# Windowed attention and retention: products of two heads of 64 issued in turn

## The chip, the cores and the metric
The kernel runs on one core of one Trainium2 chip. TensorE (PE in the profile; its loads of stationary operands are PEld) multiplies, VectorE (DVE) and ScalarE (ACT) do the elementwise work, GpSimd (POOL) some more of it, and SyncE (SP) issues the DMAs. Each engine works through its own instructions in the order in which they stand in the program. The metric is the device time of one execution, in microseconds (us).

## The reference
Two layers of a transformer block over 512 latent tokens and 256 context tokens, width 1024. A layer is a gated feed-forward, a mixer of four groups of four heads of 64 features, and a second feed-forward. The change touches two of the four groups. Group A is attention of 128 queries over the 256 context keys and a window of latent key blocks, and the context's own queries over the context keys; group C is retention in both directions:

```python
# group A, per block of 128 queries: keys of the context and of the blocks n-1, n, n+1
s = q @ k.T / 8 ; p = softmax([s, sink]) ; o = p @ v
# group C, per chunk of 128 tokens, forwards and (flipped) backwards
att = einsum('bnihd,bnjhd->bnhij', qc, kc) * d_intra[None, None]
o_intra = einsum('bnhij,bnjhe->bnihe', att, vc)
u = einsum('bnjhd,hj,bnjhe->nbhde', kc, k_w, vc)      # state after each chunk: decay * s + u
o_cross = einsum('bnihd,hi,nbhde->bnihe', qc, q_w, s_prev)
return (o_intra + o_cross), s_final
```

The last layer needs no outputs of the context stream, so it has 4 blocks of queries where the first layer has 6.

## The kernel before
The streams stay on chip by feature, so a tile of 128 partitions holds two heads of 64 features, one in partitions 0 to 63 and one in 64 to 127. Large products (feed-forwards `ul` and `y`, the mixer's projections `pj`) run as three float32r passes; the products of the heads run in float32, and the trace shows each of these as two matmul instructions.

A mixer (`mixer`) first runs retention for two pairs of heads (`group_c`, j = 0 and 1), then projects groups A and B (`proj_ab`), then runs the windowed attention of group A (`attend`), beside which nine more projections are issued, and then the recurrence of group D with group B's attention (`attend2`) in it. The order on each engine is made when the program is built: a scheduler walks the instructions by priority, which is the order of the code unless `tc.high_priority(offset=...)` shifts it, and puts projections (`pj`) between the small products where these have to wait. PSUM banks are handed out by tag (`psum`), within a tag in the order of the code: `ptr` and `ms` have one bank each in this part, `pj` three, `po` one, and `pS` holds one tile of two banks (`S`, or `ro` in retention).

In `attend` the loop is over t (two tiles of queries), blocks n, and the two heads hf of the tile. For one head: scores `S` (L1017 through the helper `mm`), maximum on DVE (L1032), exponential on ACT (L1036), scaling on DVE (L1040), transposes into `ptr` (L1047), their copy into `PT` by ACT (L1048), and then the products with the values, L1050: 4 or 5 for a latent block (the one or two neighbours, the block itself and two context blocks), 2 for a context block. They write the head's 64 partitions of the bank `w` (`po` in the rows), so each uses 64 of the array's 128 columns.

In `group_c` the loop at the end is over blocks b and the two heads e. For one head: the scores `ra` in the bank `ptr` (L1213, 64 features in, 128 columns out), their product with the decay mask `at` on DVE for both directions (L1215), and for each direction the product with the values (L1219, 128 rows in, 64 columns out) and the product of the state `St` with the weighted queries `qw` (L1221, 64 rows in, 64 columns out), both into the head's partitions of `ro`. The states come from sums `su` (L1194) in the bank `ms`, one after the other, which stand in the code ahead of this loop. The recurrence's part already has products of two heads in turn: L1117 and L1123 (`po` and `z` under L1069 in the rows) in `attend_pair`, with the same use of `high_priority`, and L595, where the two directions read partitions 0 to 63 and 64 to 127 and write two banks (tag `gr`).

Of the kernel before, what the change touches and what calls it, by code (L numbers as in the profile page):

```python
"""Two layers of a hybrid flow-matching backbone, on one core.

The streams stay on chip by feature, x[feature, token], latent tokens before context tokens. Large products
run as three float32r passes over operands split exactly into two parts of 12 bits; the others in float32.
"""
# [11 lines left out]
F32 = mybir.dt.float32  # L17
# [24 lines left out]
# how far the background work's priority lies behind that of the work around it  # L42
# [21 lines left out]
def more_constants():  # L64
# [3 lines left out]
    # rotary: partner of each feature and the sign it enters with  # L68
# [14 lines left out]
    # retention  # L83
# [18 lines left out]
    # window masks: keys of the block before, of the block after  # L102
# [11 lines left out]
class Whole:  # L114
# [20 lines left out]
    def columns(self, rows, name):  # L135
        """Rows of 128 values in DRAM, as columns on chip."""
# [44 lines left out]
    def mod_direct(self, l, b, bufs):  # L181
        """Four columns of the modulation of both streams, as rows in four groups side by side."""
# [18 lines left out]
    def mod_block(self, l, b):  # L201
        """The same, summed over rows on the vector engine."""
# [15 lines left out]
    def mod_sum(self):  # L218
        """The sum over partitions of the block before."""
# [21 lines left out]
    def scales(self, l, n, v):  # L241
        """Per feature: the norm's gain with the modulation's scale."""
        nc = self.nc
        g = self.const.tile([128, KT], F32, name=f"gs{l}{n}{v}")
        o = (3 * n + 1) * KT
        nc.vector.scalar_tensor_tensor(out=g, in0=self.mod[l][v][:, o:o + KT], scalar=1.0,
                                       in1=self.ng[:, (3 * l + n) * KT:(3 * l + n + 1) * KT], op0=ALU.add, op1=ALU.mult)
        return g
# [12 lines left out]
    def rsqrt(self, x, n, eps, op=ALU.add, scale=None):  # L261
        """(x op eps) ** -0.5 of n columns: a first guess from the bits, three steps of Newton's."""
# [16 lines left out]
    def rstd(self, segs=SEGS):  # L279
        """The rows' factors, by token."""  # L280
# [11 lines left out]
    def spread(self, pt, cols):  # L292
        """Rows of 128 tokens from columns, on all partitions or one for each 64."""
# [3 lines left out]
    def spread_rows(self, r, segs):  # L297
        """Rows over all partitions, in two banks."""
# [6 lines left out]
    def raw_open(self, l, n, shifts=True):  # L305
        """Products with modulate(rms_norm(x)) from products with x by gain: the rows' factors and the shifts enter after them.
        The shifts are two more columns, between the streams."""
# [12 lines left out]
    def raw_tile(self, k):  # L320
        """One finished tile of x by gain, in two parts of 12 bits."""
# [7 lines left out]
    def raw_rows(self, pool):  # L329
        """The rows' factors of both streams on all partitions."""  # L330
# [4 lines left out]
    def ready(self, l, n):  # L335
        """What to do with each finished tile of x before norm n of layer l."""
# [7 lines left out]
    def norm_mod(self, l, n, segs=SEGS):  # L344
        """h = modulate(rms_norm(x)), in two parts of 12 bits."""
# [15 lines left out]
    def mm3(self, outs, wh, wl, xh, xl, segs, first, last):  # L361
        """outs[i] += w.T x over segs, from parts; the low parts' product is below float32."""
# [8 lines left out]
    def split(self, raw, shape, tag, pool=None, bufs=None):  # L371
        """The two parts of a tile."""
# [8 lines left out]
    def ffn(self, l, i, segs, chunks, background, last_cb):  # L381
# [4 lines left out]
        for ci, cn in enumerate(chunks):  # L386
            gs = []
            wo = self.raw.tile([128, cn, D], F32, name="wo", tag="wo", bufs=1)
            for j in range(cn):
# [8 lines left out]
                # the first products do not wait for the shifts  # L398
# [51 lines left out]
    def gates(self, l, n, segs, half):  # L450
        """The gate columns; made once the modulation is there."""
# [8 lines left out]
    def rw_cols(self, l):  # L460
# [34 lines left out]
        # 1 - mu; 1 - k_a / 2; 2 ln_b  # L495
# [13 lines left out]
    def scan_ap(p, d, o, n, shift):  # L509
        """Tokens o to o + n, context first, in the order of direction d, or the tokens before them."""  # L510
# [33 lines left out]
    def rw_low(self, pw, pa):  # L544
        """tanh of the decays' and the inputs of the rates' low-rank part, in the order of each direction."""
# [9 lines left out]
    def rw_lengths(self, p):  # L555
        """One over the lengths of the removal keys, as columns of [block, direction, head]."""
# [18 lines left out]
    def rw_decay(self, u, p):  # L575
        """Decays, rates and removal keys of 128 tokens of each direction, for both pairs of heads."""
# [33 lines left out]
        # half the removal key of length one  # L610
# [8 lines left out]
    def rw_ops(self, u, st, p, has_r):  # L619
        """Operands of the chunks, and the products of their rows, head by head."""  # L620
# [46 lines left out]
    def rw_late(self, u, st, bon, has_r):  # L667
        """What the steps need besides the products: keys and values by token; and the bonus, in the order of the tokens."""
# [32 lines left out]
    def block(d, u):  # L701
        """The block of tokens, context first, that direction d reaches at step u."""
        return u if d == 0 else (1 - u if u < 2 else 7 - u)

    def rw_inverse(self, ops):
        """(1 - A)^-1 of every chunk, transposed, in the place of A: blocks of 16 by substitution, then twice the block beside."""
# [63 lines left out]
    def rw_step(self, ops, c, S, Y, has_r, first):  # L770
        """One chunk of both directions: its outputs, and the states after it."""
# [46 lines left out]
    def rw_norm(self, Y):  # L818
        """The head norm of each token's outputs, without its gain."""
# [10 lines left out]
    def rw_out(self, Y, u, bon):  # L830
        """Adds the normed outputs, by feature, in the order of the tokens."""
# [12 lines left out]
    def rw_scan(self, p, bon, ctx_out, first):  # L844
        """The recurrence, 128 tokens at a time; the next operands are made while a chain runs. `first` goes in after the first decays."""
# [39 lines left out]
    def psum_open(self, ctx, **tags):  # L885
        """Banks by use: within a tag they are handed out in the order of the program."""
# [3 lines left out]
    def h_open(self, n=T + 2):  # L890
        """The operands of a phase's products, by feature, in two parts: they outlive the phase that makes them."""
# [14 lines left out]
    def first_mods(self):  # L906
        """The first norm's gains, then its shifts, through buffers that are still free."""
# [16 lines left out]
    def proj(self, l, cols, both, evac):  # L924
        """128 columns of the projection (as (first, count) runs) of the latent tokens or of both streams."""
# [576 lines left out]
```

## Time and profile before
| what | value |
|---|---|
| timed runs | 3579.98 us median of 3 (3574.42 to 3582.41) |
| profiled execution | span 3572.8 us from its first to its last instruction |
| busy: PE, PEld, DVE, ACT, POOL | 3416.8 (96%), 2759.6 (77%), 2003.8 (56%), 1145.2 (32%), 168.4 (5%) us |
| chain that ended last | PE 84%, DVE 9%, ACT 3% of the span |
| mean granted TensorE clock | 0.983 |

The page gives the profiled execution's own time as its span; the timed runs also hold what lies around the span, and their fastest is 1.6 us above it, their median 7.2 us. A matmul's duration in the trace reaches from its start to its last result, and the next one starts earlier than that; so what a matmul costs TensorE is read from the distance between two starts, not from the duration.

### The profile page before, as it was taken

How to read it: one execution, taken by the hardware profiler on the slowest of the kernel's cores; microseconds unless marked ns; L12 is line 12 of the kernel's file. 1: busy time of each engine (PE TensorE's matmuls, PEld its weight loads, DVE VectorE, ACT ScalarE, POOL GpSimd, SP SyncE). 2: the span in 40 equal slices, each digit the busy share in tenths (PEclk: the TensorE clock that was granted, in tenths of full speed). 3: DMA queues.
4: the chain of work that ended last, by engine and by line, in shares of the span. 5: the costliest groups of instructions: out<-in, count | busy, mean ns of one | idle time of the engine just before them, and what ended most of it. 6: DMA issues, size and time to landing. Idle time of an engine off the chain costs nothing.

```text
span 3572.8 us, 54928 instructions
## 1 busy us (share of the span) xinstructions
PE 3416.8 (96%) x22756; PEld 2759.6 (77%) x22756; DVE 2003.8 (56%) x4351; ACT 1145.2 (32%) x2173; POOL 168.4 (5%) x350
## 2 busy tenths in 40 slices
PE   6999999999998999999999999999999988889997
PEld 5888888777775767888888888888878766557776
DVE  5766664444557856654435765553645468653333
ACT  3212212223457633221213122221424467422222
POOL 0000000000022310000000000000000023200000
PEclk8999999999999999999999999999999989999999
DMA  7443340211100014322212443330211100042330
GB/s 232 126 140 118 107 130 23 59 35 44 30 11 2 5 34 145 112 95 74 69 59 67 130 133 108 101 101 24 74 42 49 35 1 5 23 126 90 93 106 24
DMA packets 324122, 266.33 MB, mean 75 GB/s; under 512 B 27396, under 2 KB 273312, under 8 KB 323872
## 3 DMA queue, kind: packets, MB, share of 16 engines
q1 hardware_dynamic: 323872, 262.82, 24.1%
q8 instruction: 179, 2.93, 0.3%
q14 instruction: 71, 0.58, 0.1%
HBM read 260.68 MB, written 2.10 MB: 74 GB/s over the span
## 4 chain that ended last, share of the span: by engine, by line
PE 84%; DVE 9%; ACT 3%; DMA 1%; issue 1%; POOL 1%; SPq 0%; DVEq 0%; ACTq 0%; POOLq 0%
PE ul L365 12%; PE ul L369 12%; PE ul L367 12%; PE y L369 6%; PE y L367 6%; PE y L365 6%; PE pj L365 4%; PE pj L367 4%; PE pj L369 4%; PE op L1261 3%; PE S L1017 1%; PE po L1017 1%; PE ch L782 1%; DVE xtmp L725 1%; DVE w1l L378 1%
## 5 line engine op out<-in xcount | busy, mean ns | idle before, releaser
L365 PE MATMUL ul<-hh,w1h 128*128 128x512 f32 (+1 forms) x2464 | 692.8, 350 | 7.5 <-ACT w1h L377 6.7
L367 PE MATMUL ul<-hl,w1h 128*128 128x512 f32 (+1 forms) x2464 | 692.6, 348 | 0.0
L369 PE MATMUL ul<-hh,w1l 128*128 128x512 f32 (+1 forms) x2464 | 688.3, 348 | 1.3 <-DVE w1l L378 1.2
L365 PEld LDWEIGHTS ul<-hh,w1h 128*128 128x128 f32 x2464 | 395.5, 190 | 81.2 <-issue 9.9
L367 PEld LDWEIGHTS ul<-hl,w1h 128*128 128x128 f32 x2464 | 396.4, 190 | 64.0 <-issue 0.8
L369 PEld LDWEIGHTS ul<-hh,w1l 128*128 128x128 f32 x2464 | 393.4, 189 | 64.4 <-DVE w1l L378 2.8
L367 PE MATMUL y<-gl,w2h 128*128 128x512 f32 x1232 | 342.8, 347 | 4.1 <-DVE gl L431 3.8
L369 PE MATMUL y<-gh,w2l 128*128 128x512 f32 x1232 | 338.6, 346 | 5.8 <-DVE w2l L378 5.8
L365 PE MATMUL y<-gh,w2h 128*128 128x512 f32 (+1 forms) x1232 | 339.8, 346 | 0.2 <-DVE xT L445 0.2
L377 ACT ACTIVATE w1h<-w1r 128x2048 fp32r<-128x2048 f32 x88 | 168.7, 1917 | 480.2 <-PE ul L367 445.7
L215 DVE SCALAR_TENSOR_TENSOR macc<-wm,sc,macc 128x512 f32<-128x512 f32 x392 | 274.7, 749 | 75.5 <-DMA wm<-in_w_mod_dram 74.1
L445 DVE SCALAR_TENSOR_TENSOR xT<-y,gate,xT 128x512 f32<-128x512 f32 x336 | 199.4, 633 | 192.1 <-PE y L369 191.5
L377 ACT ACTIVATE w2h<-wo 128x512 fp32r<-128x512 f32 (+1 forms) x192 | 111.5, 594 | 542.6 <-PE y L367 339.8
L365 PE MATMUL pj<-hh,pwh 128*128 128x512 f32 (+2 forms) x864 | 253.7, 344 | 7.2 <-DVE qA L945 3.2
L367 PE MATMUL pj<-hl,pwh 128*128 128x512 f32 (+2 forms) x864 | 247.0, 336 | 0.0
L369 PE MATMUL pj<-hh,pwl 128*128 128x512 f32 (+2 forms) x864 | 244.9, 335 | 2.1 <-DVE pwl L378 1.9
L419 DVE TENSOR_TENSOR u<-ul,rsb 128x512 f32<-128x512 f32 (+1 forms) x132 | 70.9, 553 | 304.3 <-PE ul L369 304.3
L369 PEld LDWEIGHTS y<-gh,w2l 128*128 128x128 f32 x1232 | 194.9, 188 | 39.8 <-DVE w2l L378 10.0
L367 PEld LDWEIGHTS y<-gl,w2h 128*128 128x128 f32 x1232 | 195.4, 188 | 37.7 <-DVE gl L431 8.6
L365 PEld LDWEIGHTS y<-gh,w2h 128*128 128x128 f32 x1232 | 195.4, 188 | 36.0 <-ACT w2h L377 3.1
L378 DVE TENSOR_TENSOR w1l<-w1r,w1h 128x2048 fp32r<-128x2048 f32 x88 | 201.5, 2289 | 29.7 <-ACT w1h L377 29.7
L421 ACT ACTIVATE sg<-sg,ub 128x512 f32<-128x512 f32 (+1 forms) x132 | 74.1, 609 | 425.7 <-DVE ub L416 321.7
(355 smaller groups left out, 4576.6 us busy)
## 6 DMA issues: line engine op xcount, KB each, us to landing
w1r<-in_ffn_w_in_dram SPq DMA_DIRECT2D x176, 512.0 KB
wm<-in_w_mod_dram SPq DMA_DIRECT2D x72, 1024.0 KB
wo<-in_ffn_w_out_dram SPq DMA_DIRECT2D x88, 512.0 KB
pw<-in_w_in_dram SPq DMA_DIRECT2D x46, 512.0 KB
pw<-in_w_in_dram SPq DMA_DIRECT2D x16, 256.0 KB
wo<-in_w_out_dram SPq DMA_DIRECT2D x128, 32.0 KB
wo<-in_w_out_dram SPq DMA_DIRECT2D x64, 64.0 KB
xl<-in_x_dram SPq DMA_DIRECT2D x4, 512.0 KB
```

The lines of the kernel that those rows point to most:

```text
L215: nc.vector.scalar_tensor_tensor(out=acc[v], in0=r[:, k, :], scalar=s, in1=acc[v], op0=ALU.mult, op1=ALU.add)
L365: nc.tensor.matmul(p, lhsT=wh, rhs=xh[:, o:o + n], start=first, stop=False)
L367: nc.tensor.matmul(p, lhsT=wh, rhs=xl[:, o:o + n], start=False, stop=False)
L369: nc.tensor.matmul(p, lhsT=wl, rhs=xh[:, o:o + n], start=False, stop=last)
L377: nc.scalar.activation(out=hi, in_=raw, func=AF.Copy)
L378: nc.vector.tensor_tensor(out=lo, in0=raw, in1=hi, op=ALU.subtract)
L419: nc.vector.tensor_tensor(out=dst[:, o:o + n], in0=p, in1=self.rsb[:, o:o + n], op=ALU.mult)
L421: nc.scalar.activation(out=dst[:, o:o + n], in_=dst[:, o:o + n], func=AF.Silu, bias=b[:, u, s:s + 1])
L445: nc.vector.scalar_tensor_tensor(out=xs, in0=py[s], scalar=gt[s][:, n_:n_ + 1], in1=xs, op0=ALU.mult, op1=ALU.add)
L725: nc.vector.tensor_tensor(out=tmp[:, :, :, :n], in0=Xv[:, :, :, s:16], in1=Bv[:, :, s:16, s].unsqueeze(2).to_broadcast([128, 2, 4, n]), op ...
L1017: mm = lambda out, lt, r, st, sp: nc.tensor.matmul(out, lhsT=lt, rhs=r, start=st, stop=sp, skip_group_check=True)
L1261: nc.tensor.matmul(p, lhsT=w[i], rhs=os[i][:, osegs[i][v][0]:osegs[i][v][0] + c], start=i == 0, stop=i == m - 1)
```

## The change
In `attend` the two heads' `PT` tiles are both made first, and then the products with the values are issued block by block, head 0, head 1. In `group_c` the same is done in four steps: both heads' scores, now in two different banks (`ptr` for head 0, `ms` for head 1); both heads' masks, with four buffers `at` in place of two; the products with the values for direction 0 (head 0, head 1), then direction 1; and the products with the states in the same order. `high_priority(offset=hf)` (or `e`) brings the second head's priority forward by one place. The number of instructions on each engine stays the same. Lines of the changed kernel lie up to 15 further down (L1221 for L1213, L1231 for L1219, L1236 for L1221, L1048 for L1047).

```diff
@@ attend @@
                 if n == 0:
                     w = self.psum("po", "po")
+                pTs = []
                 for hf in range(2):
...
-                    for b, v in enumerate(vb):
-                        mm(w[rows, n * 128:(n + 1) * 128], V[:, v, rows], pT[:, b, :], b == 0, b == nb - 1)
+                    pTs.append(pT)
+                for b, v in enumerate(vb):
+                    for hf in range(2):
+                        rows = slice(64 * hf, 64 * hf + 64)
+                        with self.tc.high_priority(offset=hf):
+                            mm(w[rows, n * 128:(n + 1) * 128], V[:, v, rows], pTs[hf][:, b, :], b == 0, b == nb - 1)
@@ group_c @@
-                for e in range(2):
-                    r = slice(64 * e, 64 * e + 64)
-                    pt = self.psum("ra", "ptr")
-                    nc.tensor.matmul(pt[:, :128], lhsT=k[r, cs], rhs=q[r, cs], start=True, stop=True)
-                    at = ap.tile([128, 2, 128], F32, name="at", tag="at", bufs=2)
-                    nc.vector.tensor_tensor(out=at, in0=pt[:, :128].unsqueeze(1).to_broadcast([128, 2, 128]), in1=self.dm[:, 2 * j + e], op=ALU.mult)
-                    for d in range(2):
-                        w = po[r, d, b * 128 - o_:(b + 1) * 128 - o_]
-                        s = state[d].get(b)
-                        nc.tensor.matmul(w, lhsT=V[:, b, r], rhs=at[:, d, :], start=True, stop=s is None, skip_group_check=True)
-                        if s is not None:
-                            nc.tensor.matmul(w, lhsT=s[r], rhs=qw[d][r, cs], start=False, stop=True, skip_group_check=True)
+                hs = [(e, slice(64 * e, 64 * e + 64)) for e in range(2)]
+                pts = [self.psum("ra", tag) for tag in ("ptr", "ms")]
+                for e, r in hs:
+                    with self.tc.high_priority(offset=e):
+                        nc.tensor.matmul(pts[e][:, :128], lhsT=k[r, cs], rhs=q[r, cs], start=True, stop=True)
+                ats = []
+                for e, r in hs:
+                    at = ap.tile([128, 2, 128], F32, name="at", tag="at", bufs=4)
+                    nc.vector.tensor_tensor(out=at, in0=pts[e][:, :128].unsqueeze(1).to_broadcast([128, 2, 128]), in1=self.dm[:, 2 * j + e], op=ALU.mult)
+                    ats.append(at)
+                ws = lambda r, d: po[r, d, b * 128 - o_:(b + 1) * 128 - o_]
+                for d in range(2):
+                    for e, r in hs:
+                        with self.tc.high_priority(offset=e):
+                            nc.tensor.matmul(ws(r, d), lhsT=V[:, b, r], rhs=ats[e][:, d, :], start=True, stop=b not in state[d], skip_group_check=True)
+                for d in range(2):
+                    for e, r in hs:
+                        if b in state[d]:
+                            with self.tc.high_priority(offset=e):
+                                nc.tensor.matmul(ws(r, d), lhsT=state[d][b][r], rhs=qw[d][r, cs], start=False, stop=True, skip_group_check=True)
```

The scheduler's order moves with it. The first place is TensorE in retention of the first layer, pair j = 0, blocks 2 and 3 of the latent tokens. Before (each `at_` number is one head of one block; a row without xN is one product):

```order
L1213 MATMUL ra_5728<-q_5261,k_5262 128x128
L369 MATMUL pj_5957<-hh_116,pwl_5954 128x512
L369 MATMUL pj_5958<-hh_116,pwl_5954 128x258
L365 MATMUL pj_5957<-hh_116,pwh_5953 128x512
L365 MATMUL pj_5958<-hh_116,pwh_5953 128x258
L1219 MATMUL ro_5695<-at_5730,V_5482 64x128
L1221 MATMUL ro_5695<-qw0_5631,St_5653 64x128
L1219 MATMUL ro_5695<-at_5730,V_5482 64x128
L1221 MATMUL ro_5695<-qw1_5632,St_5653 64x128
L1213 MATMUL ra_5736<-q_5261,k_5262 128x128
```

The same blocks on TensorE in the changed program (`at_5732` and `at_5734` are the two heads of block 2, `at_5748` and `at_5750` those of block 3):

```order
L1221 MATMUL ra_5745<-q_5261,k_5262 128x128
L1221 MATMUL ra_5744<-q_5261,k_5262 128x128
L1231 MATMUL ro_5695<-at_5732,V_5482 64x128
L1231 MATMUL ro_5695<-at_5734,V_5482 64x128
L1231 MATMUL ro_5695<-at_5732,V_5482 64x128
L1231 MATMUL ro_5695<-at_5734,V_5482 64x128
L1236 MATMUL ro_5695<-qw0_5631,St_5653 64x128 x2
L1236 MATMUL ro_5695<-qw1_5632,St_5653 64x128 x2
L1231 MATMUL ro_5695<-at_5748,V_5482 64x128
L1231 MATMUL ro_5695<-at_5750,V_5482 64x128
```

The projections that stood behind each `ra` are gone from these blocks; they stand ahead of and behind the four latent blocks now, and the heads alternate. Over both layers the 80 products L1219 stood one by one between products of other shapes (72 runs of one, 4 runs of two of the same head, where there is no state yet); now 16 stand alone, 12 runs have two (one of each head) and 10 have four. The 72 products L1221 also stood one by one; now 4 runs have two and 16 have four. Of the 40 scores, 28 stand alone and 6 pairs stand together. A passage from `pj` (or another product of the full array) into these shapes stood 53 times and stands 24 times.

The second place is TensorE in the windowed attention of the first layer, t = 0, block 1 of the latent tokens, five key blocks. Before, the first head's products, one run (the second head has such a run of its own behind its transposes):

```order
L1047 MATMUL ptr_7270<-ident_67,P_7257 128x128
L1017 MATMUL po_7200<-PT_7263,kv0_5184 64x128 x5
L1017 MATMUL S_7307<-kv0_5184,qA0_5185 128x256
L1017 MATMUL S_7307<-kv0_5184,qA0_5185 128x384
L1047 MATMUL ptr_7293<-ident_67,P_7286 128x128 x4
```

In the changed program one product of head 0 (`PT_7263`) stands alone behind that head's last transpose, and the other nine stand behind the last transpose of head 1 (`PT_7287`):

```order
L1048 MATMUL ptr_7294<-ident_67,P_7281 128x128
L1018 MATMUL po_7200<-PT_7287,kv0_5184 64x128
L1018 MATMUL po_7200<-PT_7263,kv0_5184 64x128
L1018 MATMUL po_7200<-PT_7287,kv0_5184 64x128
L1018 MATMUL po_7200<-PT_7263,kv0_5184 64x128
L1018 MATMUL po_7200<-PT_7287,kv0_5184 64x128
L1018 MATMUL po_7200<-PT_7263,kv0_5184 64x128
L1018 MATMUL po_7200<-PT_7287,kv0_5184 64x128
L1018 MATMUL po_7200<-PT_7263,kv0_5184 64x128
L1018 MATMUL po_7200<-PT_7287,kv0_5184 64x128
L365 MATMUL pj_7934<-hh_116,pwh_7929 128x258
```

Over both layers the 160 products stood in 48 runs of one head; now they stand in 20 runs of one, 4 of three, 8 of seven and 8 of nine, the heads in turn.

## Rows read from the trace of the kernel before

**Rows 1.** The page: span, busy time by engine, the last chain by engine.

```profile
span 3572.8 us, 54928 instructions
...
PE 3416.8 (96%) x22756; PEld 2759.6 (77%) x22756; DVE 2003.8 (56%) x4351; ACT 1145.2 (32%) x2173; POOL 168.4 (5%) x350
...
PE 84%; DVE 9%; ACT 3%; DMA 1%; issue 1%; POOL 1%; SPq 0%; DVEq 0%; ACTq 0%; POOLq 0%
```

**Rows 2.** Windows: retention, then attention with projections, of each layer; busy us, clock.

```profile
core 0: us, PE busy (x) PEld busy (x) DVE busy (x) ACT busy (x) POOL busy (x), PEclk, DMA share, GB/s
625.00:840.00 215.00, 210.67 (x1165) 159.82 (x1164) 102.33 (x248) 58.22 (x94) 2.48 (x8) 1.00 0.15 42
840.00:1045.00 205.00, 203.34 (x1157) 157.29 (x1156) 107.37 (x306) 86.46 (x191) 7.40 (x32) 0.99 0.12 34
2555.00:2720.00 165.00, 162.09 (x1005) 128.88 (x1004) 82.82 (x208) 47.21 (x82) 1.09 (x27) 1.00 0.19 49
2720.00:2870.00 150.00, 148.17 (x940) 119.55 (x939) 79.48 (x237) 68.74 (x145) 5.26 (x7) 1.00 0.13 35
```

**Rows 3.** Timeline, TensorE, retention: start, length, products (two passes each).

```profile
718.04 0.48 PE L1213 MATMUL ra<-q,k 64*128 64x128 f32 x2
718.45 0.51 PE L365 MATMUL pj<-hh,pwh 128*128 128x512 f32 x1
718.79 0.39 PE L367 MATMUL pj<-hl,pwh 128*128 128x512 f32 x1
719.03 0.39 PE L369 MATMUL pj<-hh,pwl 128*128 128x512 f32 x1
719.34 0.43 PE L1219 MATMUL ro<-at,V 128*64 128x128 f32 x2
719.71 0.43 PE L1221 MATMUL ro<-qw,St 64*64 64x128 f32 x2
720.07 0.43 PE L1219 MATMUL ro<-at,V 128*64 128x128 f32 x2
720.43 0.43 PE L1221 MATMUL ro<-qw,St 64*64 64x128 f32 x2
720.79 0.49 PE L1213 MATMUL ra<-q,k 64*128 64x128 f32 x2
```

**Rows 4.** Timeline, TensorE, windowed attention: runs of four and of five products.

```profile
926.56 1.09 PE L1017 MATMUL po<-PT,kv 128*64 128x128 f32 x8
927.58 0.39 PE L365 MATMUL pj<-hh,pwh 128*128 128x258 f32 x1
...
932.60 1.31 PE L1017 MATMUL po<-PT,kv 128*64 128x128 f32 x10
933.84 0.39 PE L365 MATMUL pj<-hh,pwh 128*128 128x258 f32 x1
```

**Rows 5.** Timeline, TensorE, group B: windows to 1104.05, to 1104.10, then whole.

```profile
1103.90 0.33 PE L1069 MATMUL z<-ident,rc 128*64 128x128 f32 x2
...
1103.90 0.44 PE L1069 MATMUL z<-ident,rc 128*64 128x128 f32 x4
...
1103.90 0.98 PE L1069 MATMUL z<-ident,rc 128*64 128x128 f32 x13
1104.61 0.38 PE L1069 MATMUL po<-PT,VB 128*64 128x256 f32 x1
```

**Rows 6.** Timeline, TensorE, recurrence: 64-row products of two directions; 64-row, 64-column ones.

```profile
1155.91 0.37 PE L595 MATMUL wa<-ta,rw 64*128 64x128 f32 x1
1155.92 0.37 PE L595 MATMUL wa<-tw,rw 64*128 64x128 f32 x1
1156.12 0.27 PE L595 MATMUL wa<-ta,rw 64*128 64x128 f32 x1
...
1127.62 0.68 PE L782 MATMUL ch<-R,G 64*64 64x64 f32 x16
```

**Rows 7.** Groups by line: the work on DVE and ACT between the products.

```profile
L378 DVE TENSOR_TENSOR pwl<-pw,pwh 128x1024 fp32r<-128x1024 f32 x54 | 65.8, 1219 | 1.3 <-ACT pwh L377 1.2
L1048 ACT COPY PT<-ptr 128x512 f32<-128x512 f32 (+2 forms) x56 | 25.9, 463 | 83.9 <-PE ptr L1047 83.9
L1215 DVE TENSOR_TENSOR at<-ra,k_ret 128x256 f32<-128x256 f32 x40 | 17.0, 424 | 61.7 <-PE ra L1213 56.2 <-PE ro L1219 5.3
```

**Rows 8.** Timeline, DVE, retention: the mask behind the scores of 718.04.

```profile
718.56 0.42 DVE L1215 TENSOR_TENSOR at<-ra,k_ret 128x256 f32<-128x256 f32 x1 [1.70 <-PE ra L1213]
```

## The prediction
> **What bounds the kernel now.** The page comes first: TensorE is busy for 96% of the span and makes 84% of the chain that ended last [rows 1]. Then the windows of the stages that the change touches: over the four stretches of retention and windowed attention TensorE is busy 724 of 735 us at a granted clock of 0.99 to 1.00, which is the upper of its two levels, while VectorE is busy about half of the time and ScalarE a third [rows 2]. The reader is to see that these stages are bound by TensorE's stream: projections `pj` fill what the small products leave, so every stretch of TensorE time taken out of the small products brings all that follows forward, as long as TensorE doesn't wait instead. Last comes the timeline, where starts are compared.
>
> **What a small product costs now.** In retention a product with the values starts at 719.34, one with the state at 719.71, the next at 720.07 and 720.43, the next score at 720.79: 0.36 us each. A score takes 0.41 (718.04 to 718.45) [rows 3]. In attention a run of four products of one head takes 1.02 us (926.56 to 927.58), one of five 1.24 (932.60 to 933.84) [rows 4]; the difference is 0.218 for one more product, 0.109 for each of its two passes, and a run of n costs 0.36 + 0.218 (n - 1). So 0.14 of a product that stands alone goes into changing the array's shape and starting up, and 0.22 into its passes.
>
> **What two heads in turn cost.** The kernel already has such products. In `z` two passes have started by 1104.05, four by 1104.10, and thirteen lie between 1103.90 and the next `po` at 1104.61 [rows 5]. Two passes of one product are at least 0.109 apart in the serial runs, so the two that start together are those of two heads; then come 0.71 us with six more steps, 0.16 for the first and 0.11 for each of the rest. A step holds a pass of both heads. So a run of n products in turn costs 0.36 + 0.109 (n - 2) for an even n and 0.36 + 0.109 (n - 1) for an odd one, whose last product has no partner. That is for 128 rows by 64 columns, the shape of both products with the values. For 64 rows by 64 columns, the shape of the state's products, sixteen passes end within 0.68 us, of which the last one's length is some 0.2: about 0.06 for each pair of passes of 64 columns [rows 6], so they overlap too. For 64 rows by 128 columns, the scores' shape, the two directions start 0.01 apart at 1155.91 and again at 1156.12, into two banks [rows 6]; the scores now also have two banks.
>
> At this place a rule of the Trainium skill speaks for less. TensorE: Matmul & The Clock Gate, section Part 3: Packing small matmuls, says of matmuls of tiles of the array that they start and end strictly in program order. Were the two passes of a product two places in that order, then a head's second pass would stand ahead of the other head's first, and an even run would cost one step more. The trace has two starts together and the next two 0.16 later, against that reading; what it would change is a rival below.
>
> **The sum**, from the runs counted in the order of before and of the change:
> - Products with the values in retention: before 72 runs of one at 0.36 and 4 serial runs of two at 0.58, 28.2 us; now 28 runs of one or two at 0.36 and 10 of four at 0.58, 15.9. Gain 12.3.
> - Products with the state: before 72 at 0.36, 25.9; now 4 runs of two at 0.36 and 16 of four at 0.58, 10.7. Gain 15.2.
> - Scores: 40 at 0.41, 16.4; now 28 alone and 6 pairs, a pair at the price of one, 13.9. Gain 2.5. Most scores stay apart, since the second head's bank `ms` is handed out behind the state sums.
> - Attention: before 48 runs with 160 products, 48 x 0.36 + 112 x 0.218 = 41.7; now 20 x 0.36, 4 x 0.58 (three), 8 x 1.01 (seven) and 8 x 1.23 (nine), 27.5. Gain 14.2.
> - Passages into these shapes: the projection ahead of one takes 0.31 (719.03 to 719.34) instead of 0.24 [rows 3]. There are 29 fewer in retention and none fewer in attention: 29 x 0.07, gain 2.0. If the longer projection behind one (718.45 to 718.79, 0.34) goes as well, 0.17 each, 4.9. I take 2.0, since the first projection behind a run will still be there after fewer, longer runs.
>
> Gain in TensorE time 46.2 us. Nothing is added on VectorE, ScalarE or the queues: the same instructions, in another order.
>
> **New waits** are the price that the trace doesn't show. In retention the projections behind each score are gone, so what covers the mask is the block before. The mask starts 0.52 after its score (718.04 to 718.56) and takes 0.42 [rows 8]; the second head's follows with another 0.42, 1.36 in all. Between a pair of scores and the products that use them stand, for block 3, the scores themselves (0.41), a run of four with the values and one of four with the state (0.58 each): 1.57. That covers it by 0.2, and only if VectorE is free; a split of projection weights (L378, 1.219 us [rows 7]) in between would leave some 1.0 of waiting with nothing but the same chain queued behind. One such split in each of the four passes over j and layer makes 4 us. In attention, all but one of a pair's products now come after the second head's transposes; the last needs the copy of the last transposed block (0.46 at the mean, L1048 [rows 7]), which nine products in turn (0.16 + 7 x 0.109 = 0.92 to the last start) still cover; where the copy stands behind an exponential it will be late, and I put 0.1 on each of 20 pairs, 2 us. The bounds are 0 and 16 (two splits in each pass, 8, and 0.4 for each of 20 pairs, 8); I take 6, nearer to nothing because the four stretches now show only 735 - 724 = 11 us of idle TensorE [rows 2]. What follows, the remaining projections and then the recurrence, stands behind the same engine and moves forward by the gain: in the order of the changed program more than 50 projection instructions still stand between the last product of attention and the recurrence, so the chain of softmax doesn't become the end.
>
> So TensorE's stream shortens by 40 us: the profiled span goes from 3572.8 to about 3533, and the median, 7.2 above the span, from 3580 to **3540 us**.
>
> **Rivals.**
> - *The passes go in program order.* Every even run costs a step more: 22 with the values and 20 with the state at 0.109, 4.6, and some 1.0 on the pairs of scores. Gain 34 to 35, 3545 us. For it is only the rule above; against it are the starts of [rows 5].
> - *The waits take a good part.* The upper bound of 16 and as much again, because the dense blocks' round trip is not covered once VectorE is late: gain 14 to 30, 3550 to 3566 us. For it: TensorE runs its stream in order, and four latent blocks of retention now stand with hardly a projection between. Against it: VectorE is busy about half of the time in retention [rows 2].
> - *The change doesn't do what it says*: the heads don't overlap here, only the shape changes less often. Then runs cost 0.36 + 0.218 (n - 1): values 22.9 (gain 5.3), state 18.6 (7.3), pairs of scores 1.2, attention 40 runs, 40.6 (1.1), passages 2.0. Gain 17, 3563 us. Against it are [rows 5] and [rows 6], both with the same shapes.
> - *Slower.* The second head's score in `ms` waits behind other users of that bank, and each block's round trip is exposed whole, with a split ahead of the masks: 1.36 + 1.22 = 2.6 us in each of 20 blocks, 52 us, against 46 gained: 3586 us. It decides from 2.3 us of new waiting for every block. The order has the block before between scores and products, so this needs VectorE blocked at every block, which its 102 busy us of 215 make unlikely [rows 2].
>
> **How the numbers follow.** A measurement of this kernel tells about 0.2% (7 us) from no change. The forecast has 0.55, program order 0.10, the waits 0.17, no overlap 0.10, slower 0.03, and 0.05 is left for a gain that is given back later, in the recurrence. Range: from 3526 (46.2 and the 2.9 of the other passages, no waits, 4 us for the spread of the runs) to 3563 (no overlap, and most of the case of waits). Faster: all cases but the last two, 0.92; same 0.05; slower 0.03.
>
> **What would show it.** In the profile of the changed kernel: pairs of `ro` and of `po` passes that start within 0.01 us; a run of four with the state over 0.58 us, one of nine with the values over 1.23; fewer TensorE microseconds between the stages' first and last products, 30 in retention and 14 in attention; idle time ahead of L1231 and L1018 of some 6 us in all. The prediction is wrong if runs of four take near 1.02 (no overlap), if TensorE shows idle time for `at` at most blocks, or if the recurrence starts earlier but ends as late as now.

## The result, and the profile after

| what | changed kernel | before, same chip |
|---|---|---|
| timed runs | 3531.5 us median of 4 (3529.93 to 3532.26) | 3577.2 us median of 4 (3572.06 to 3582.41) |
| ratio | 0.9875, 95% interval 0.9861 to 0.9889 | |
| profiled execution | span 3529.8 us, its own time 3531.58 | span 3572.8 |
| mean granted clock | 0.982 | 0.983 |

The change makes the kernel 1.25% faster, 45.7 us between the medians and 43.0 between the two spans. The page of the changed kernel, in the rows that answer to [rows 1]:

```profile
span 3529.8 us, 54945 instructions
...
PE 3372.1 (96%) x22756; PEld 2738.7 (78%) x22756; DVE 2002.2 (57%) x4351; ACT 1145.6 (32%) x2173; POOL 166.6 (5%) x350
...
PE 84%; DVE 10%; ACT 3%; DMA 1%; issue 1%; POOL 1%; SPq 0%; DVEq 0%; ACTq 0%; POOLq 0%
```

TensorE loses 44.7 us of busy time with the same number of matmuls. Its weight loads (PEld), which overlap them, lose 20.9, and the other engines stay within 2 us. The windows of the four stretches, cut about where the same stages now lie, answer to [rows 2]:

```profile
core 0: us, PE busy (x) PEld busy (x) DVE busy (x) ACT busy (x) POOL busy (x), PEclk, DMA share, GB/s
623.00:813.00 190.00, 187.05 (x1136) 148.30 (x1134) 99.50 (x240) 56.66 (x93) 2.35 (x8) 1.00 0.18 47
813.00:1020.00 207.00, 203.00 (x1193) 157.66 (x1194) 109.69 (x316) 89.60 (x194) 7.43 (x32) 0.98 0.12 34
2533.00:2663.00 130.00, 127.62 (x893) 106.72 (x893) 70.35 (x188) 40.35 (x73) 0.27 (x6) 1.00 0.19 50
2663.00:2830.00 167.00, 165.44 (x1077) 133.48 (x1075) 93.90 (x261) 77.63 (x161) 7.93 (x34) 1.00 0.15 42
```

The stretches now take 694 us instead of 735, and TensorE idles for 694 - 683.1 = 10.9 us of them, where it idled for 10.7. The cuts are round numbers; from the start of the first score of retention to the start of the last product of attention with the values the two layers took 323.6 and 260.6 us before (689.3 to 1012.9 and 2581.4 to 2842.0), and take 298.2 and 239.3 now (689.1 to 987.3 and 2559.6 to 2798.9). That is 46.7 us less, with 6.7 us of idle TensorE for 7.6. What was taken out of the stream came out of the time, and no idle time took its place in these stages; of the 46.7, 3.7 are lost again in the rest of the program. These two stretches, "first score to last product", come back below.

The next view is TensorE's timeline in the dense blocks of retention, which answers to [rows 3]. The two rows at 780.05 are answers for windows up to 780.06 and up to 780.9, the two at 784.17 up to 784.19 and up to 785.2; so the first of each pair shows what had started by then.

```profile
779.43 0.27 PE L1231 MATMUL ro<-at,V 128*64 128x128 f32 x1
779.64 0.48 PE L1221 MATMUL ra<-q,k 64*128 64x128 f32 x2
780.05 0.33 PE L1231 MATMUL ro<-at,V 128*64 128x128 f32 x2
...
780.05 0.44 PE L1231 MATMUL ro<-at,V 128*64 128x128 f32 x4
780.42 0.65 PE L1236 MATMUL ro<-qw,St 64*64 64x128 f32 x8
781.00 0.37 PE L1221 MATMUL ra<-q,k 64*128 64x128 f32 x1
...
784.17 0.38 PE L1221 MATMUL ra<-q,k 64*128 64x128 f32 x2
...
784.17 0.49 PE L1221 MATMUL ra<-q,k 64*128 64x128 f32 x4
784.60 0.66 PE L1231 MATMUL ro<-at,V 128*64 128x128 f32 x8
785.18 0.33 PE L1236 MATMUL ro<-qw,St 64*64 64x128 f32 x2
```

Two passes have started by 780.06, so a pair starts within 0.01. A run of four products with the state goes from 780.42 to 781.00, 0.58 us; one of four with the values from 784.60 to 785.18, 0.58. A pair of scores, four passes, goes from 784.17 to 784.60, 0.43, little more than one score alone (0.41). In attention a run of nine takes 1.24 us (905.02 to 906.26), which is what five took before [rows 4]:

```profile
905.02 1.31 PE L1018 MATMUL po<-PT,kv 128*64 128x128 f32 x18
906.26 0.39 PE L365 MATMUL pj<-hh,pwh 128*128 128x258 f32 x1
```

The groups by line show the same products with the idle time ahead of them at the end:

```profile
L1018 PE MATMUL po<-PT,kv 128*64 128x128 f32 x320 | 30.4, 282 | 0.1
L1231 PE MATMUL ro<-at,V 128*64 128x128 f32 x160 | 18.8, 292 | 0.0
L1225 DVE TENSOR_TENSOR at<-ra,k_ret 128x256 f32<-128x256 f32 x40 | 16.0, 421 | 19.2 <-PE ra L1221 19.2
```

Ahead of the products with the values TensorE waits 0.0 us in retention and 0.1 in attention. The mask is as long as before (421 ns for 424 in [rows 7]).

### The profile page after: what moved, and what is told of

Same layout as the page of the kernel before. It is cut to its first block, busy times and chain, and to the rows that moved or that the text cites. A ratio compares the mean times of both kernels' runs of the same rounds, so it can differ in the third digit from the quotient of the medians.

```text
span 3529.8 us, 54945 instructions
## 1 busy us (share of the span) xinstructions
PE 3372.1 (96%) x22756; PEld 2738.7 (78%) x22756; DVE 2002.2 (57%) x4351; ACT 1145.6 (32%) x2173; POOL 166.6 (5%) x350
## 4 chain that ended last, share of the span: by engine, by line
PE 84%; DVE 10%; ACT 3%; DMA 1%; issue 1%; POOL 1%; SPq 0%; DVEq 0%; ACTq 0%; POOLq 0%
PE ul L365 13%; PE ul L369 13%; PE ul L367 13%; PE y L369 6%; PE y L367 6%; PE y L365 6%; PE pj L365 4%; PE pj L367 4%; PE pj L369 4%; PE op L1276 3%; PE S L1018 1%; PE ch L782 1%; DVE xtmp L725 1%; DVE w1l L378 1%; PE po L1018 1%
```

## Experiments

The theories are A, a step of the array holds a pass of both heads; B, the runs are only longer and the shape changes less often; C, waits for the second head take the gain; and, from the first runs on, D and E on which products may overlap (E says that only neighbours in program order do; D is worked out below). Times of "products" below are worked out from the starts of all TensorE rows of a timeline, each product counted up to the next start; only the profile gives them, and they repeat to 0.1 us in two profiles of the changed kernel.

**Each half of the change alone.** Attention alone keeps `group_c` of before, retention alone keeps `attend` of before, each as in the diff above.

> The alternation in windowed attention alone; retention as before. Theory A (a step of the array holds a pass of both heads): the order of the 160 products is that of the changed kernel, so they shorten from 41.7 to 27.5 us, and with no new waits the time falls by 14 us, from 3577 to about 3563. Rival B (no overlap, only fewer changes of the array's shape): 1.1 us, about 3576. Rival C (waits on the second head's copies): each us of idle TensorE ahead of the products with the values is taken from the 14.

> The alternation in retention alone; windowed attention as before. Theory A: scores, products with the values and products with the state shorten by 2.5 + 12.3 + 15.2 = 30.0 us, about 3547. Rival B: 1.2 + 5.3 + 7.3 = 13.8, about 3563. If the two halves of the change add up, the gains of this kernel and of the one with attention alone make the 45.7 us of the whole; if the end of the mixer gives a fixed part back, their sum differs from it by some us.

Attention alone: 3568.92 us, ratio 0.9963 (0.9949 to 0.9977). Its products go from 41.9 to 27.6 us, 14.3 less. Retention alone: 3543.76 us, ratio 0.9888 (0.9875 to 0.9901); products with the state 25.9 to 10.8, with the values 28.4 to 16.1, scores 16.6 to 14.1, 29.9 less in all. Theory B gave 1.1 and 13.8, and falls. The halves add up in the products (14.3 + 29.9 = 44.2, as in the whole) and from first score to last product (11.6 + 34.9 = 46.5 us less, the whole 46.7). By the ratios they gain 13 and 40, more than the whole; but these runs had different granted clocks, with which the time goes (below). Among runs at a mean granted clock of 0.982 the four of before have a mean of 3577.6, attention alone 3566.2 (two), retention alone 3544.8 (one), the whole 3531.3 (three): 11.4 + 32.8 = 44.2 against 46.3, which agree within the 4 us by which the four of before differ.

**All products behind the second head, in turn and head by head.** In the first kernel the second head's product leads, and the rest of the block is tied behind it, so that no product stands alone:

```diff
-                    for hf in range(2):
+                    for hf in (1, 0):
...
+                            if (b, hf) != (0, 1):
+                                es.enter_context(self.tc.issue_after(lead.ins))
+                            es.enter_context(self.tc.high_priority(offset=1 - hf))
+                            lead = mm(w[rows, n * 128:(n + 1) * 128], V[:, v, rows], pTs[hf][:, b, :], b == 0, b == nb - 1)
```

and the same for the products with the values in `group_c`; those with the state are tied behind them, each behind the one before. The second kernel differs from it in the order of the loops over heads and blocks (in retention over heads and directions), and in attention it also leaves out `high_priority`.

> The changed kernel with the second head's product ahead in each pair and all products of a block behind it in turn, so that none stands alone: in attention runs of 4, 8, 8 and 10 (20 in all, 20.1 us for 27.5), in retention 20 runs of four with the values (11.6 for 15.9); products with the state as in the changed kernel, and one pair of scores more (0.4). Theory A: 12.1 us less than the changed kernel, about 3519, if the wait for the second head stays covered. Rival C (waits): the first product of each of 40 blocks now waits for the second head's mask or copy; at 0.3 to 0.4 for each that takes the 12 to 16 us back, 3531 to 3536, with idle time ahead of these products in the profile.

> The same places as the kernel with the second head ahead, but head by head within each block (both products of one head with the values, then both of the other; the state's the same; in attention all of one head, then all of the other): as many changes of the array's shape in retention, eight more in attention, and no alternation. Theory A: a run of n costs 0.36 + 0.218 (n - 1), less one overlap where the two heads meet; against the kernel with the second head ahead 20 us more if they overlap there, 34 if not, so 3539 to 3553. Rival B (only the number of changes of shape counts): within 2 us of the kernel with the second head ahead, about 3520.

With the second head ahead: 3525.5 us, ratio 0.9841 (0.9826 to 0.9856). By the ratios that is 12 us less than the changed kernel, as theory A gave, though the time itself, on another chip, is only 6 less. The products of attention take 20.5 us (20.1 expected), those with the values 11.7 (11.6), and the wait that theory C feared isn't there: 0.2 us ahead of the products of attention, 0.0 in retention. So the wait for the second head is covered even when the whole block waits for it.

Head by head: 3535.37 us, ratio 0.9868 (0.9848 to 0.9888), 9.9 more than with the second head ahead, and here neither theory was right. Theory B falls again, since attention costs 12.0 us more (32.5 for 20.5) with only eight runs more (28 for 20), which at 0.14 each are 1.1. But in retention head by head costs nothing: products with the values 11.9 us for 11.7, with the state 10.9 for 10.8. The timeline shows why, first a run of two products of each head, then one of four of each; rows with the same start are answers for windows that end later (at 932.87 and 933.6, at 895.79, 895.85 and 897.2):

```profile
932.85 0.34 PE L1018 MATMUL po<-PT,kv 128*64 128x128 f32 x2
...
932.85 0.66 PE L1018 MATMUL po<-PT,kv 128*64 128x128 f32 x8
933.45 0.48 PE L1018 MATMUL S<-kv,qA 64*128 64x256 f32 x1
...
895.30 0.65 PE L1018 MATMUL po<-PT,kv 128*64 128x128 f32 x4
...
895.30 0.82 PE L1018 MATMUL po<-PT,kv 128*64 128x128 f32 x6
...
895.30 1.58 PE L1018 MATMUL po<-PT,kv 128*64 128x128 f32 x16
896.81 0.70 PE L1018 MATMUL S<-kv,qA 64*128 64x256 f32 x2
```

Two and two take 0.60 us, as in turn (0.58): two passes have started within 0.02, though the second head's first product stands third in the order. Four and four take 1.51, between the 1.02 of strict turn and the 1.89 of eight in series (0.36 + 7 x 0.218): up to 0.49 only four passes have started, the first head's first two products, and then two start within 0.06. Passes of one half are at least 0.1 apart, so these two are of two heads: the second head's first product, fifth in the order, starts with the third, 0.22 ahead of where the fourth can. Start by start, the sixteen passes form two trains of eight, in steps of 0.11 (the first step of each is 0.16), and the second train begins 0.49 behind the first. From that comes theory D: one product may wait for its half of the array while products of the other half behind it start; a second one that must wait holds up all behind it.

**Groups of two and of three.** The kernel with the second head ahead, with attention's products in groups:

```diff
-                for b, v in enumerate(vb):
-                    for hf in (1, 0):
+                seq = [(b, hf) for b0 in range(0, nb, 2) for hf in (1, 0) for b in range(b0, min(b0 + 2, nb))]
+                for i, (b, hf) in enumerate(seq):
...
```

and with 3 for 2.

> The kernel with the second head ahead, but in attention two products of one head, then two of the other. Theory D (one instruction may wait for its half of the array, and one for the other half that stands behind it still starts; a second one of the same half holds up all behind it): full overlap, a run of eight 1.02 us and one of ten 1.24, 20.5 us in all as in strict turn. Theory E (only neighbours in program order overlap): one overlap in three is lost, a run of eight some 1.4, 27 us in all.

> The same with three products of one head, then three of the other, then the rest. Theory D: the first product of the other half starts when the second of the first half does, some 0.22 to 0.27 later, and the run ends later by as much: 16 runs of eight and ten longer by some 0.22, 24 us in all for 20.5. If more than one instruction may wait for its half, no loss, 20.5 us; if only neighbours overlap, 30 us or more, like the kernel head by head (32.5).

One run each, 3522.22 and 3526.34 us, so only their profiles can decide. Groups of two: 21.3 us in attention (20.5 expected by D); theory E, 27, falls. Groups of three: 25.0 (24 expected by D, 30 or more by neighbours alone, 20.5 with room for more than one). A run of four and four in groups of two, and in groups of three (answers for windows that end at 894.25, 894.32 and 895.4):

```profile
895.44 1.14 PE L1018 MATMUL po<-PT,kv 128*64 128x128 f32 x16
896.51 0.48 PE L1018 MATMUL S<-kv,qA 64*128 64x256 f32 x1
```

```profile
894.03 0.43 PE L1018 MATMUL po<-PT,kv 128*64 128x128 f32 x2
...
894.03 0.60 PE L1018 MATMUL po<-PT,kv 128*64 128x128 f32 x4
...
894.03 1.36 PE L1018 MATMUL po<-PT,kv 128*64 128x128 f32 x16
895.32 0.48 PE L1018 MATMUL S<-kv,qA 64*128 64x256 f32 x1
```

1.07 and 1.29 us beside 1.02 in turn. In groups of three only two passes, one product, start in the first 0.22; then the second product of that head and the first of the other start within 0.07. Theory D fits both, with up to 0.05 more than it gave.

**The cover of the wait taken away.** Two buffers `at` in place of four:

```diff
-                    at = ap.tile([128, 2, 128], F32, name="at", tag="at", bufs=4)
+                    at = ap.tile([128, 2, 128], F32, name="at", tag="at", bufs=2)
```

> The changed kernel with two buffers for the masked scores instead of four, so that the masks of a block wait until the products of the block before are done: the cover of the wait is taken away. In its order more products stand alone: with the values 42 runs of one or two and 8 of three or four, 19.8 us for 15.9, scores four pairs fewer, 1.6. Order alone: 5.5 us more than the changed kernel, about 3537. Theory C (the round trip of a block is what the block before covers, as the prediction priced it): up to 1 us of idle TensorE in each of 20 blocks on top, about 3547 to 3557, ahead of the products with the values. If the scheduler's other products cover it anyway, 3537 and no idle time there.

3548.1 us, ratio 0.9912 (0.9890 to 0.9935): by the ratios 13 us worse than the changed kernel, and 12.7 from first score to last product. Theory C gave up to 1 us of idle TensorE at each block; the groups of this kernel show none:

```profile
L1231 PE MATMUL ro<-at,V 128*64 128x128 f32 x160 | 23.5, 295 | 0.0
```

The loss is in the stream: products with the values 20.0 us for 16.1, scores 15.7 for 14.1, and 7.9 us in the projections, which the scheduler put into the gaps: 57 passages from a projection into one of these shapes instead of 42, and 68 instead of 52 back. Of the 7.9, 1.5 are idle time behind projections. So in this kernel a missing cover turns mainly into shorter runs; the time came out where theory C had it, but by another way, and the "order alone" expectation had the runs and forgot the projections.

**The second head's score in another bank.** Retention takes the bank of attention's products, `po`, for it instead of `ms`; first on top of the kernel with the second head ahead, then alone.

```diff
-                pts = [self.psum("ra", tag) for tag in ("ptr", "ms")]
+                pts = [self.psum("ra", tag) for tag in ("ptr", "po")]
```

> The kernel with the second head ahead, and in retention the second head's score in the bank of the products with the values of attention, which is free there, instead of the one behind the state sums: 14 pairs of scores and 12 alone instead of 7 and 26, 2.9 us less; products with the state in 12 runs of four and 12 of two instead of 16 and 4, 0.6 more; with the values 0.3 more. About 2 us less than the kernel with the second head ahead, 3523 where that took 3525, if the second head's score and mask bring no new wait; 3531 or more if the blocks now stand so close that masks are waited for.

> The changed kernel with only the bank of the second head's score changed: by its order scores 0.8 less, products with the values 2.7 less, products with the state 3.5 more, so nothing in sum, 3531 within the spread of single runs. If the bank alone made the gain of the kernel that has both edits, some 5 us less.

With both edits: 3520.55 us, ratio 0.9835 (0.9813 to 0.9856); scores 10.9 us (13.7 with the second head ahead alone), state 11.4, values 12.1. Against the kernel with the second head ahead alone (0.9841) the intervals don't tell it apart. The bank alone: 3542.77 us in one run, 12 more than expected. Its products are as counted (scores and values 3.5 less, state 3.4 more). Against the changed kernel, 4 us more lie between first score and last product, and 9 in the unchanged recurrence of the second layer, which took 328 us in this profile and 319 in that of the changed kernel, at the lower granted clock shown at the end. A time from one run can't decide an effect of this size.

**The changed kernel and the best one on one chip.**

> The changed kernel once more, beside the kernels below on one chip: 0.9875 of the time before again, within 0.002; and a second profile of it, for what the first showed only once: 1220 us from the last product of the output projection of the first layer to the first score of retention in the second, against 1215 in the one profile of before. If that was given back because of the change, it is 1219 to 1220 again and about 1215 in before alone; if it is the clock's spread from one execution to the next, this or another profile lies near 1215.

> The kernel with the second head ahead and the second score bank once more, beside the changed kernel on one chip: 10 to 14 us less than that, as the runs of products count out (attention 7.1, values 4.0, scores 3.2 less, state 0.6 and the rest of the passages the other way).

Changed kernel: 3535.07 us (3531.46 to 3539.81), ratio 0.988 (0.986 to 0.9899). Second head ahead with the other bank: 3518.43 us (3516.20 to 3522.62), ratio 0.9831 (0.9812 to 0.9851). It beats both kernels: every run of it is below the fastest of the changed kernel, and the medians are 16.6 us apart, where 10 to 14 were expected. Products make 13.8 of it; from first score to last product it is 13.4.

## Why the prediction was right, point by point

**The four terms of products came out to a tenth.** Gains in us, predicted and worked out from the starts in the profiles of before and of the changed kernel:

| term | predicted | measured |
|---|---|---|
| products with the values, retention | 12.3 | 12.3 |
| products with the state | 15.2 | 15.1 |
| scores | 2.5 | 2.5 |
| products of attention | 14.2 | 14.3 |
| passages, as the time of all projections | 2.0 | 0.4 in the first profile, 2.0 in the second |
| new waits ahead of these products | -6 (0 to 16) | -0.1 |

The step of 0.109 us for a pass of both heads, read from `z` and from serial runs [rows 4, 5], was right for all of them, the 64 by 64 shape included (0.58 for four). The term of the passages is not measured well: two profiles of one program differ by 1.6 us in it. From first score to last product 46.7 us went, 44.2 of them in these products and 0.9 in idle time; the remaining 1.6, with twelve projection instructions more in the stretch than before, is of the size of this term. The prediction counted no fewer passages into attention's products; the trace has 39 there instead of 46, besides 24 instead of 53 in retention.

**Passes in program order** was a rival. The Trainium skill, TensorE: Matmul & The Clock Gate, Part 3: Packing small matmuls, says that matmuls of tiles start and end strictly in program order. The run of four and four head by head disagrees: the fifth product's first pass starts at 0.49 us with the third's, before the fourth. A product of one half overtakes a waiting product of the other. And an even run costs no extra step: four with the values take 0.58, where this rival had 0.69.

**The alternation was not what retention needed.** The prediction derived the pairs from two heads in turn. Head by head within a block is as fast there; what gained 27.4 us is that both heads' products stand in one run, with at most two of a head behind each other, and overlap there. In attention, with four and five products of a head, the alternation is worth 12.0 us of 21.4 that are to be had.

**The new waits were mis-sized: 6 us at the products, measured 0.1.** The price stood for a split of weights between a score and its products, and for late copies of `PT`; neither shows. The waiting that the change does bring stands elsewhere, at the head norm's row factors `rv`. The waits of TensorE at that tile, changed kernel:

```profile
PE rv L295 <- ACT rb L980: 2.3, 2, 1.3
PE rv L295 <- DVE oc L1251: 0.5, 1, 0.5
PE rv L295 <- DVE od L1251: 0.5, 1, 0.5
```

The columns are us in total, times, longest. 3.3 us in all; before and in the kernel with attention alone there is none at this tile, with retention alone 3.2. So it belongs to the change of retention. Why is open: if denser products left the norm's chain on VectorE and ScalarE less to hide behind, the kernel with the second head ahead, with still denser ones, should wait longer there, and it waits 1.9. 2.5 us of waits of `pj` for `rsb` of before are gone in the same profile, so the sum is small.

**Some of the gain was given back where nothing was changed.** The last product of the output projection of the first layer comes 26.3 us earlier (1339.8 for 1366.1), the first score of retention in the second layer only 21.8. That stretch took 1215.3 us in the one profile of before and 1219.8 and 1219.5 in the two of the changed kernel. A part of it is the passage into the FFN, in windows of 34 us from that product on, before and changed (columns as in the windows above):

```profile
1366.00:1400.00 34.00, 28.34 (x154) 24.12 (x153) 20.30 (x37) 11.36 (x13) 0.00 (x0) 0.90 0.81 243
```

```profile
1340.00:1374.00 34.00, 28.61 (x140) 24.61 (x140) 18.21 (x33) 10.08 (x11) 0.00 (x0) 0.80 0.77 232
```

A mean of 0.90 is 6.8 us at 1.2 GHz and the rest at 2.4, one of 0.80 is 13.6 us: 6.8 us more at half speed are worth 3.4 us, by this estimate. In both profiles the clock falls where TensorE waits for the rows' sums and then for the first weights of the FFN: before in the second of these waits (0.72 from 1370 to 1374), in the changed kernel in the first (0.50 from 1343 on). In the changed kernel TensorE then also waits for one more part of the weights. Before:

```profile
1369.45 1.50 PE L285 MATMUL ssps<-mean,ss 128*128 128x1 f32 x12 [2.98 <-DVE ss L259]
1373.60 1.01 PE L365 MATMUL ul<-hh,w1h 128*128 128x512 f32 x2 [2.65 <-ACT w1h L377]
```

Changed:

```profile
1343.12 2.72 PE L285 MATMUL ssps<-mean,ss 128*128 128x1 f32 x12 [2.98 <-DVE ss L259]
1347.33 1.01 PE L365 MATMUL ul<-hh,w1h 128*128 128x512 f32 x2 [1.49 <-ACT w1h L377]
...
1350.55 1.01 PE L369 MATMUL ul<-hh,w1l 128*128 128x512 f32 x2 [0.93 <-DVE w1l L378]
```

Whether the change causes it stays open. The two profiles of the best kernel, the same program, have 1216.4 us (0.85 in that window) and 1219.2 (0.80), so one program shows both; attention alone has 1220.4. Three kernels that hold the change (second head ahead, head by head, groups of two) have 0.90 in their windows, as before, and still take 1217.8 to 1219.5, so the clock in this window is not all of it. And the low 1215 of before was seen once; there is no second profile of it.

The median of 3531.5 lies 8.5 below the forecast. Of that, 2.8 is the kernel before, whose median of four is 3577.2 where the forecast started from 3580; 5.7 is a larger gain, 45.7 for 40, about the 6 of the waits that weren't there. Between the two profiles the gain is 43.0: there the 4.5 us given back, which the prediction had only among its small chances, take most of the 6 us that the missing waits had left. The 2.7 between 43.0 and 45.7 are spread between executions, so it is in part luck that the medians come so near to the sum without waits (46.2). On a second chip the ratio was 0.988, a gain of 44 us.

## What to carry to other kernels

Where products fill half of the array, put the two halves' products into one run, with at most two of the same half behind each other; strict turn is the safe form and matters from three on. Let the half that is ready last lead, so that none of the others runs alone: a product alone cost 0.36 us here, one more in a run in turn 0.109. Price a missing cover in the scheduler's order as well as in idle time: here it showed as projections between shorter runs. The waits that the change did bring, 3.3 us, stood at the head norm, not where the heads were joined.

## What the runs showed of the hardware that was not expected

**Products overtake across halves, with room for one that waits.** Four and four head by head take 1.51 us, in groups of three 1.29, in groups of two 1.07, in turn 1.02. The program's order, in which each engine was said to work, so holds on TensorE within one half of the array, and not across the two. Theory D came from the first of these runs and gave the next two beforehand; another rule that fits all four is not ruled out.

**The spread between executions goes with the granted clock.** 29 runs of the kernel before go from 3569.33 us at a mean granted clock of 0.984 to 3589.80 at 0.978; a straight line through them loses 2.7 us for each 0.001, and the other kernels' runs give 1.7 to 2.8. A part of it sits in the recurrence of the second layer. The same work there in the changed kernel, with attention alone, and in the changed kernel with the other bank:

```profile
2793.00:3112.00 319.00, 286.95 (x3466) 204.28 (x3464) 220.36 (x687) 184.02 (x481) 70.13 (x125) 0.94 0.07 19
```

```profile
2831.00:3156.00 325.00, 292.56 (x3465) 209.28 (x3463) 220.13 (x687) 184.03 (x481) 69.68 (x125) 0.92 0.07 18
```

```profile
2795.00:3123.00 328.00, 296.53 (x3468) 213.30 (x3467) 220.53 (x687) 183.80 (x481) 70.04 (x125) 0.90 0.07 18
```

VectorE and ScalarE do the same work in all three; TensorE is idle for some 32 us of each, in many short waits, and the more of the stretch runs at 1.2 GHz the longer it is: the idle time stays, the busy time grows. Why the clock falls more often in one execution than in the next is open. Comparing runs at one granted clock brought the sum of the two halves above nearer to the whole than the ratios did.
